# Gate1's and scale2's modulation moved from the heads to the first projections, with the first heads' parts in other buffers

## The chip, the core and the metric

The kernel runs on one core of a Trainium2 chip. The metric is the time of one execution in microseconds of the device. Matrix products run on TensorE (PE in the rows), with the weight loads as a row of their own (PEld); elementwise work runs on VectorE (DVE) and ScalarE (ACT); SyncE (SP) issues the DMAs.

## What is computed

One trunk layer over 512 positions of 1024 channels, in float32: two parallel branches, a merge by learned gates, and a squared-ReLU MLP. A modulation vector of six parts is computed from `c` first.

```python
mod = (c_act @ w_ada[l] + b_ada[l])[:, None, :]
shift1, scale1, gate1, shift2, scale2, gate2 = jnp.split(mod, N_MOD, axis=-1)

h = rms_norm(x) * (1.0 + scale1) + shift1
proj = h @ w_in[l]
xr, gr, q, k, v, gm = jnp.split(proj, [o1, o2, o3, o4, o5], axis=-1)
xr = causal_depthwise_conv(xr, conv_w[l], conv_b[l])
y_rnn = rg_lru(xr, ...) * jax.nn.gelu(gr)
q = apply_rope(rms_norm(q) * q_norm_gain[l], cos, sin)
k = apply_rope(rms_norm(k) * k_norm_gain[l], cos, sin)
y_attn = diff_attention(q, k, v, lam, subln_gain[l], lam_init)

gates = jax.nn.sigmoid(gm).reshape(B, S, N_BRANCH, D_MODEL)
merged = gates[:, :, 0] * (y_rnn @ w_proj_rnn[l]) + gates[:, :, 1] * (y_attn @ w_proj_attn[l])
x = x + gate1 * (merged @ w_out[l])
h2 = rms_norm(x) * (1.0 + scale2) + shift2
ff = jnp.square(jax.nn.relu(h2 @ w_ff1[l])) @ w_ff2[l]
x = x + gate2 * ff
```

Shift1 and scale1 are needed for the very first product, gate1 only behind `w_out`, scale2 only behind that.

## The kernel before

Everything is kept with channels on the 128 partitions and the 512 positions along the row, or the other way round for queries, keys and values. A float32 product is made of three products of a high part and a low part: `load_w` (L114) loads a 128x1024 block of weights (512 KB, DMA on SP), ScalarE casts it to the high part `wh` (L122), VectorE subtracts to get the low part `wl` (L123), and `mm3` (L127) issues three matmuls of 512 columns (L129, L130, L131) for each 128x128 block. One such block of weights, called a unit here, is 24 matmuls.

The stages, in the order in which they run: the x-branch `xr` (7 blocks in seven banks at once, then `xr7`), with shift1 and scale1 computed beside it by `ada_halves`; the first quarter of queries and keys (`qk_quarter(0)`, four units, which serves heads 0 and 1); the gelu gates `gr`, eight units, with the convolutions beside them; the first half of the values (`v_half(0)`, four units) with the RG-LRU gates (`gates`, L433, matmuls on `xch`, `xcl` into two banks `pg0`, `pg1`) and the transposes of the first queries and keys (`qk_transpose(0)`) between; then the heads. `heads()` yields after each small step of the attention, and `fill()` walks `PLAN`, in which letters stand for units: `g`, `m` merge gates (`gm`), `s` the scans, `q`, `t` further quarters of queries and keys, `v` the other values, `p` the products with `w_proj_rnn`. Behind them stand `pa` (the attention's projection), `wo`, and the MLP.

A column of the modulation vector is a dot product on VectorE of 1024 weights per partition with `c`. `ada_chunk(j, k)` (L184) does it with one instruction (L188) on a tile of 128x1024 in the pool "w" of 3 buffers, which the weights use too. `ada_halves(j, k)` (L191) does it with two instructions (L200), one behind the other, on tiles of 128x512 with tag "q" (12 buffers), in which from the gates on the parts of queries and keys live. `ADA` is (2, 4): part 2 is gate1, part 4 is scale2. `fill()` issues `ada_chunk(2, n)` with each step `p` and `ada_chunk(4, n)` with each step `m`; parts 3 and 5 have their own place beside `pa` and in the MLP.

`qk_transpose` makes for each of four groups a bank by four transposes, a high part `qh` (ScalarE, L549) and a low part `ql` (VectorE), and DMAs copy the halves of both to `qs`, `kh` and `kl` (L555, L556, L562, L563). A buffer of `qh` or `ql` is free again when its copies have landed. Both take tag "t" (4 buffers), which `xch` and `xcl` of the gates take too. Tag "a" has 6 buffers; `ig` of the gates (L445) and the attention's tiles take it. The banks `pg0`, `pg1` have tag "sc" (2 buffers), which the scores of the attention take too.

The order on each engine is made by a scheduler that goes by the order of the code and by its own estimates of when an instruction can start; the cast and the subtraction of `load_w` are put ahead of other work by `tc.high_priority(HP)`. So an instruction that is moved in the code can shift others on every engine.

Of the kernel before, what the change touches and what calls it, by code (L numbers as in the profile page):

```python
# [17 lines left out]
F32R = mybir.dt.float32r  # L18
# [9 lines left out]
KC = D // P  # L28
# [13 lines left out]
ADA = (2, 4)  # L42
# [11 lines left out]
def build(tc, out, x, xT_in, c, pos, vecs, reps, ada, w_xr, w_xr7, w_qk, w_v, w_gr, w_gm, w_lru,  # L54
# [4 lines left out]
    with ExitStack() as es:  # L59
# [11 lines left out]
        def slot(tag, bufs, name, dt=F32):  # L71
            return (big if tag in "mh" else mix).tile([P, S], dt, name=name, tag=tag, bufs=bufs)

        def t_(name, dt=F32, tag="t"):
            return (tmp if tag == "t" else mix).tile([P, S], dt, name=name, tag=tag,
                                                     bufs=dict(t=B_T, a=B_A, r=B_R)[tag])
# [31 lines left out]
        def f32(t):  # L108
            return t.bitcast(F32)
# [32 lines left out]
        def split_l(dst, src, h):  # L142
            return nc.vector.tensor_tensor(dst, src, f32(h), op=ALU.subtract)
# [40 lines left out]
        def ada_chunk(j, k):  # L184
            col = j * 8 + k
            w = wpool.tile([P, D], F32, name=f"ada{col}", tag="w", bufs=3)
            nc.sync.dma_start(w, ada[j, k])
            nc.vector.tensor_tensor_reduce(w, w, cb, 1.0, bada[:, col:col + 1], op0=ALU.mult,  # L188
                                           op1=ALU.add, accum_out=mod[:, col:col + 1])
# [234 lines left out]
        def conv(n):  # L424
            cw = lambda j: vec[:, V_CW + n * 4 + j:V_CW + n * 4 + j + 1]
            xc = slot("y", B_Y, f"xc{n}")
            nc.scalar.activation(xc, xr[n], AF.Identity, bias=vcol(V_CB, n), scale=cw(3))
            for sft in (1, 2, 3):
                nc.vector.scalar_tensor_tensor(xc[:, sft:], xr[n][:, :S - sft], cw(3 - sft), xc[:, sft:],
                                               op0=ALU.mult, op1=ALU.add)  # L430
            return xc

        def gates(n, xc, prev):  # L433

            xh = t_(f"xch{n}", F32R)
            nc.scalar.copy(xh, xc)
            xl = t_(f"xcl{n}", F32R)
            split_l(xl, xc, xh)
            c0 = slice(n % 4 * P, (n % 4 + 1) * P)
            pg = [bank(f"pg{j}_{n}", "sc", 2) for j in range(2)]  # L440
            for j in range(2):
                mm3(pg[j], wg[j][n // 4][0][:, c0], wg[j][n // 4][1][:, c0], xh, xl, True, True)
            r = slot("y", B_Y, f"r{n}")
            after(nc.scalar.activation(r, pg[0], AF.Sigmoid, bias=vcol(V_BA, n)), prev)
            ig = t_(f"ig{n}", tag="a")  # L445
            after(nc.scalar.activation(ig, pg[1], AF.Sigmoid, bias=vcol(V_BX, n)), prev)
            nc.vector.tensor_tensor(xc, ig, xc, op=ALU.mult)
            th = slot("m", B_M, f"th{n}")
            last = nc.scalar.activation(th, r, AF.Tanh, scale=sp4[:, n:n + 1])
            return r, xc, th, last  # L450
# [28 lines left out]
        def run(gen):  # L479
            while True:  # L480
                try:
                    next(gen)
                except StopIteration as e:
                    return e.value
# [24 lines left out]
        def qk_quarter(qt):  # L509

            pss = yield from token_major(w_qk[qt], f"qk{qt}_")
            s2 = tiny(f"qs{qt}", 32)
            rot = []
            v4 = lambda t: t.rearrange("p (m g d) -> p m g d", m=2, g=4)
            g8 = lambda t: t.rearrange("p (a b) -> p a b", b=64)
            for t in range(TB):
                raw = t_(f"raw{qt}_{t}", tag="r")
                nc.scalar.copy(raw, pss[t])
                rot.append(raw)
            for t in range(TB):  # L520
                raw = rot[t]
                sqt = t_(f"qsq{qt}_{t}", tag="r")
                nc.scalar.activation(sqt, raw, AF.Square)
                nc.vector.tensor_reduce(s2[:, t * 8:t * 8 + 8], g8(sqt), axis=AX.X, op=ALU.add)
                r4, s4 = v4(raw), v4(sqt)
                for hf in range(2):
                    a, b = slice(hf * 32, hf * 32 + 32), slice(32 - hf * 32, 64 - hf * 32)
                    nc.vector.tensor_tensor(s4[:, :, :, a], r4[:, :, :, b],
                                            st[:, t, :, None, a].to_broadcast([P, 2, 4, 32]), op=ALU.mult)
                nc.vector.tensor_tensor(r4, r4, ct[:, t, :, None, :].to_broadcast([P, 2, 4, 64]), op=ALU.mult)  # L530
                nc.vector.tensor_tensor(raw, raw, sqt, op=ALU.add)
            rq = tiny(f"rq{qt}", 32)
            rsqrt(rq, s2, 32, 1.0 / 64, EPS, f"rq{qt}")
            for t in range(TB):
                nc.vector.tensor_tensor(g8(rot[t]), g8(rot[t]),
                                        rq[:, t * 8:t * 8 + 8, None].to_broadcast([P, 8, 64]), op=ALU.mult)
            return rot

        def qk_transpose(qt, rot):


            res = []
            half = [slice(0, 64), slice(64, 128)]
            for j in (0, 2, 1, 3):
                pt = bank(f"qT{qt}_{j}", "tp", 1)
                for t in range(TB):
                    nc.tensor.transpose(pt[:, t * P:(t + 1) * P], rot[t][:, j * P:(j + 1) * P], ident)
                th = t_(f"qh{qt}_{j}", F32R)
                nc.scalar.copy(th, pt)  # L549
                tl = t_(f"ql{qt}_{j}", F32R)  # L550
                split_l(tl, pt, th)
                for m in range(2):
                    if j < 2:
                        st_ = slot("q", B_Q, f"qs{qt}_{j}_{m}", F32R)
                        nc.sync.dma_start(f32(st_)[half[0]], f32(th)[half[m]])  # L555
                        nc.sync.dma_start(f32(st_)[half[1]], f32(tl)[half[m]])  # L556
                        res.append(st_)
                    else:
                        pair = []
                        for x_, nm_ in ((th, "kh"), (tl, "kl")):  # L560
                            st_ = slot("q", B_Q, f"{nm_}{qt}_{j}_{m}", F32R)
                            nc.sync.dma_start(f32(st_)[half[0]], f32(x_)[half[m]])  # L562
                            nc.sync.dma_start(f32(st_)[half[1]], f32(x_)[half[m]])  # L563
                            pair.append(st_)
                        res.append(pair)
            return [((res[0], res[1]), (res[2], res[3])), ((res[4], res[5]), (res[6], res[7]))]
# [82 lines left out]
        xr = [evac_xr(n, xr_ps[n]) for n in range(NK)]  # L649
        xr.append(evac_xr(NK, project(w_xr7, h, "xr7")))  # L650
        wg = lru_weights()
        qk0 = run(qk_quarter(0))
        gel, xcs = [], []
        for n in range(KC):
            gel.append(gelu_block(n))
            xcs.append(conv(n))
        lg = []
        gv = v_half(0)
        for n in range(KC):
            if n % 2 == 0:  # L660
                next(gv)
            lg.append(gates(n, xcs[n], gel[-1][1]))
            if n == QT0:
                qk0 = qk_transpose(0, qk0)
        v0 = run(gv)
# [19 lines left out]
        def fill():  # L685

            rot = {}
            for group in PLAN.split("/"):
                for op in group.split():
                    o, n = op[0], int(op[1:])  # L690
                    if o == "g":
                        gate0(n)
                    elif o == "s":
                        hs = lru_scan(n, lg[n][0], lg[n][1], sqs[-1])
                        yr.append(y_rnn(n, hs, gel[n][0]))
                    elif o == "q":
                        rot[n] = yield from qk_quarter(n)
                    elif o == "t":
                        qks[n] = qk_transpose(n, rot.pop(n))
                    elif o == "v":  # L700
                        vs[n] = yield from v_half(n)
                    elif o == "p":
                        proj_rnn(n)
                        ada_chunk(ADA[0], n)
                    elif o == "m":
                        th1.append(gate(KC + n, slot("y", B_Y, f"thg{KC + n}")))
                        ada_chunk(ADA[1], n)
                if o not in "qv":
                    yield

# [48 lines left out]
        for n in range(KC):  # L759
            pp = project(w_pa[n], y_att, f"pa{n}")  # L760
            ada_chunk(3, n)
            th = t_(f"mg{n}")
# [12 lines left out]
        for n in range(KC):  # L775
# [3 lines left out]
            t = slot("m", B_M, f"x1_{n}")  # L779
# [47 lines left out]
        for k in range(KC):  # L827
            t = t_(f"h2f{k}")
# [278 lines left out]
```

## Time and profile before

| | us |
|---|---|
| runs | 893.14, 896.8, 897.4 |
| median | 896.8 |
| profiled execution | 894.77 |
| its span in the trace | 893.0 |
| PE busy | 867.7 (97%) |
| DVE busy | 657.4 (74%) |
| ACT busy | 448.3 (50%) |

The span is the time from the first to the last recorded instruction; 1.8 us of the profiled execution lie around it. The rows use the engine names above; a name such as `pg<-xch,wgh` is the output and the inputs of an instruction, without buffer numbers. A bracket at the end of a row, `[2.06 <-ACT xch L436]`, says that the engine stood idle for 2.06 us before it, and what ended the wait. Times in rows are counted from the start of the span.

### The profile page before, as it was taken

How to read it: one execution, taken by the hardware profiler on the slowest of the kernel's cores; microseconds unless marked ns; L12 is line 12 of the kernel's file. 1: busy time of each engine (PE TensorE's matmuls, PEld its weight loads, DVE VectorE, ACT ScalarE, POOL GpSimd, SP SyncE). 2: the span in 40 equal slices, each digit the busy share in tenths (PEclk: the TensorE clock that was granted, in tenths of full speed). 3: DMA queues.
4: the chain of work that ended last, by engine and by line, in shares of the span. 5: the costliest groups of instructions: out<-in, count | busy, mean ns of one | idle time of the engine just before them, and what ended most of it. 6: DMA issues, size and time to landing. Idle time of an engine off the chain costs nothing.

```text
span 893.0 us, 11189 instructions
## 1 busy us (share of the span) xinstructions
PE 867.7 (97%) x4012; PEld 707.0 (79%) x4012; DVE 657.4 (74%) x1227; ACT 448.3 (50%) x748; POOL 2.2 (0%) x40
## 2 busy tenths in 40 slices
PE   6999999999999999999999999989999999999988
PEld 3888888687878878877778888878888888888867
DVE  6972983499969855895868566879646883876597
ACT  6663544895536533534543343746545544553541
POOL 0000000000000000000000000000000000000000
PEclk9999999999999999999999999999999999999999
DMA  8932236321255474448745332772421342233002
GB/s 318 353 142 97 92 116 144 120 70 48 95 127 158 137 213 146 142 136 206 246 155 183 135 119 78 273 237 95 163 99 48 118 142 95 72 117 118 1 1 94
DMA packets 54874, 121.56 MB, mean 136 GB/s; under 512 B 5666, under 2 KB 23202, under 8 KB 54820
## 3 DMA queue, kind: packets, MB, share of 16 engines
q1 hardware_dynamic: 54820, 120.87, 41.9%
q8 instruction: 31, 0.51, 0.2%
q14 instruction: 23, 0.19, 0.1%
HBM read 106.17 MB, written 2.10 MB: 121 GB/s over the span
## 4 chain that ended last, share of the span: by engine, by line
PE 74%; DVE 16%; DMA 5%; ACT 2%; issue 2%; SPq 0%; DVEq 0%; ACTq 0%
PE f L129 5%; PE f L130 5%; PE f L131 5%; DMA ada<-in_ada 3%; DVE wl L123 3%; PE X L131 3%; PE X L130 3%; PE X L129 3%; PE qk L131 2%; PE qk L129 2%; PE qk L130 2%; PE xr L129 2%; PE xr L131 2%; PE xr L130 2%; PE wo L130 2%
## 5 line engine op out<-in xcount | busy, mean ns | idle before, releaser
L122 ACT CAST wh<-w 128x1024 fp32r<-128x1024 f32 (+1 forms) x113 | 117.9, 1043 | 214.6 <-issue 56.2
L123 DVE TENSOR_TENSOR wl<-w,wh 128x1024 fp32r<-128x1024 f32 (+1 forms) x113 | 137.0, 1213 | 87.7 <-ACT wh L122 86.6
L129 PE MATMUL f<-h2h,wh 128*128 128x512 f32 x240 | 93.0, 390 | 2.3 <-ACT wh L122 2.3
L131 PE MATMUL f<-h2h,wl 128*128 128x512 f32 x240 | 93.5, 390 | 0.4 <-DVE wl L123 0.4
L130 PE MATMUL f<-h2l,wh 128*128 128x512 f32 x240 | 93.2, 389 | 0.0
L129 PEld LDWEIGHTS f<-h2h,wh 128*128 128x128 f32 x240 | 45.1, 188 | 12.0 <-ACT wh L122 2.7
L131 PEld LDWEIGHTS f<-h2h,wl 128*128 128x128 f32 x240 | 45.1, 188 | 10.0 <-DVE wl L123 0.8
L188 DVE CUSTOM_DVE_ANT_0 ada<-ada,cb,bada 128x1024 f32<-128x1024 f32 x32 | 41.0, 1281 | 16.1 <-DMA ada<-in_ada 16.1
L130 PEld LDWEIGHTS f<-h2l,wh 128*128 128x128 f32 x240 | 45.1, 188 | 9.3
L131 PE MATMUL gm<-hh,wl 128*128 128x512 f32 x128 | 51.3, 401 | 0.0
L129 PE MATMUL gm<-hh,wh 128*128 128x512 f32 x128 | 51.1, 399 | 0.0
L130 PE MATMUL gm<-hl,wh 128*128 128x512 f32 x128 | 50.9, 398 | 0.0
L129 PE MATMUL qk<-wh,hh 128*128 128x512 f32 x128 | 50.8, 398 | 0.0
L131 PE MATMUL qk<-wh,hl 128*128 128x512 f32 x128 | 50.6, 395 | 0.0
L130 PE MATMUL qk<-wl,hh 128*128 128x512 f32 x128 | 50.2, 393 | 0.0
L588 ACT ACTIVATE e<-e,nm 128x128 f32<-128x128 f32 (+3 forms) x64 | 35.8, 561 | 28.7 <-DVE nm L586 28.4
L905 DVE TENSOR_TENSOR p_1l<-b,p_1h 128x1024 fp32r<-128x1024 f32 x27 | 33.0, 1223 | 21.8 <-ACT p_1h L904 21.8
L904 ACT CAST p_0h<-b 128x1024 fp32r<-128x1024 f32 x27 | 28.5, 1054 | 27.2 <-PE X L131 14.0
L904 ACT CAST p_1h<-b 128x1024 fp32r<-128x1024 f32 x27 | 28.3, 1050 | 27.3 <-PE f L130 24.5
L905 DVE TENSOR_TENSOR p_0l<-b,p_0h 128x1024 fp32r<-128x1024 f32 x27 | 33.0, 1222 | 11.7 <-ACT p_0h L904 11.6
L948 DVE TENSOR_TENSOR b<-b,b 128x1024 f32<-128x1024 f32 x32 | 38.7, 1220 | 0.1
L586 DVE CUSTOM_DVE_ANT_0 e<-sc,mask 128x128 f32<-128x128 f32 (+3 forms) x64 | 30.3, 486 | 10.4 <-PE sc L581 10.4
(438 smaller groups left out, 2169.8 us busy)
## 6 DMA issues: line engine op xcount, KB each, us to landing
ada<-in_ada SPq DMA_DIRECT2D x32, 512.0 KB, 4.2
w<-in_w_ff SPq DMA_DIRECT2D x32, 512.0 KB, 3.2
b<-in_w_ff SPq DMA_DIRECT2D x32, 512.0 KB, 3.5
ada<-in_ada SPq DMA_DIRECT2D x32, 256.0 KB, 5.8
w<-in_w_qk SPq DMA_DIRECT2D x16, 512.0 KB, 3.3
w<-in_w_gm SPq DMA_DIRECT2D x16, 512.0 KB, 3.6
w<-in_w_gr SPq DMA_DIRECT2D x8, 512.0 KB, 3.2
w<-in_w_v SPq DMA_DIRECT2D x8, 512.0 KB, 3.2
```

Source lines behind the costliest of these rows:

```text
L122: i_w = nc.scalar.copy(wh[:, :n], w[:, :n])
L123: nc.vector.tensor_tensor(wl[:, :n], w[:, :n], f32(wh)[:, :n], op=ALU.subtract)
L129: nc.tensor.matmul(ps, lh, rh, start=first, stop=False, skip_group_check=more)
L130: nc.tensor.matmul(ps, lh, rl, start=False, stop=False, skip_group_check=more)
L131: nc.tensor.matmul(ps, ll, rh, start=False, stop=last, skip_group_check=more)
L188: nc.vector.tensor_tensor_reduce(w, w, cb, 1.0, bada[:, col:col + 1], op0=ALU.mult, op1=ALU.add, accum_out=mod[:, col:col + 1])
L586: nc.vector.tensor_tensor_reduce(e[:, :n], ps[m][:, :n], mask[:, S - n:], 1.0, 1e30, op0=ALU.add, op1=ALU.min, accum_out=nm)
L588: nc.scalar.activation(e[:, :n], e[:, :n], AF.Exp, bias=nm, scale=-1.0, accum_out=sums[:, m:m + 1])
L904: nc.scalar.copy(v4(wh), v)
L905: nc.vector.tensor_tensor(v4(wl), v, f32(v4(wh)), op=ALU.subtract)
L948: nc.vector.tensor_tensor(d, d, s_, op=ALU.add)
```

## The change

Three edits. `qk_transpose(0)` takes `qh` and `ql` of the first quarter from tag "a" instead of "t". The sixteen `ada_chunk` calls in `fill()` go. In their place stand `ada_halves(2, 0..7)`, two beside each of the four units of the first queries and keys, `ada_halves(4, 0..3)` beside the units 4 to 7 of `gr`, and `ada_halves(4, 4..7)` behind the first gates. Sixteen instructions of 128x1024 become 32 of 128x512, and sixteen DMAs of 512 KB become 32 of 256 KB, all in buffers of tag "q".

```diff
--- before.py
+++ after.py
@@ -545,9 +545,10 @@
                 pt = bank(f"qT{qt}_{j}", "tp", 1)
                 for t in range(TB):
                     nc.tensor.transpose(pt[:, t * P:(t + 1) * P], rot[t][:, j * P:(j + 1) * P], ident)
-                th = t_(f"qh{qt}_{j}", F32R)
+                tag = "t" if qt else "a"
+                th = t_(f"qh{qt}_{j}", F32R, tag)
                 nc.scalar.copy(th, pt)
-                tl = t_(f"ql{qt}_{j}", F32R)
+                tl = t_(f"ql{qt}_{j}", F32R, tag)
                 split_l(tl, pt, th)
                 for m in range(2):
                     if j < 2:
@@ -649,17 +650,27 @@
         xr = [evac_xr(n, xr_ps[n]) for n in range(NK)]
         xr.append(evac_xr(NK, project(w_xr7, h, "xr7")))
         wg = lru_weights()
-        qk0 = run(qk_quarter(0))
+        qk0 = qk_quarter(0)
+        for n in range(4):
+            next(qk0)
+            for i in range(2):
+                ada_halves(ADA[0], 2 * n + i)
+        qk0 = run(qk0)
         gel, xcs = [], []
         for n in range(KC):
             gel.append(gelu_block(n))
             xcs.append(conv(n))
+            if n >= 4:
+                ada_halves(ADA[1], n - 4)
         lg = []
         gv = v_half(0)
         for n in range(KC):
             if n % 2 == 0:
                 next(gv)
             lg.append(gates(n, xcs[n], gel[-1][1]))
+            if n == 0:
+                for i in range(4, KC):
+                    ada_halves(ADA[1], i)
             if n == QT0:
                 qk0 = qk_transpose(0, qk0)
         v0 = run(gv)
@@ -701,10 +712,8 @@
                         vs[n] = yield from v_half(n)
                     elif o == "p":
                         proj_rnn(n)
-                        ada_chunk(ADA[0], n)
                     elif o == "m":
                         th1.append(gate(KC + n, slot("y", B_Y, f"thg{KC + n}")))
-                        ada_chunk(ADA[1], n)
                 if o not in "qv":
                     yield
 
```

The line numbers behind L547 are higher by one in the changed kernel up to L652. In the order of the instructions a name such as `pg1_3` has a block's number, and a bracket says which semaphores an instruction waits for.

**PE, values and gates.** Before the change, all matmuls of the gates 2 and 3 (`pg0_2` to `pg1_3`) stand together behind the last row of the values `v0_3`, and `gm0`, the first merge gate, follows:

```order
L131 MATMUL v0_3_1268<-wh24_1547,hl7_558 128x512
L129 MATMUL pg0_2_1443<-xch2_1439,wgh0_0_756 128x512 [waits Activation_49]
L129 MATMUL pg1_2_1444<-xch2_1439,wgh1_0_766 128x512
L130 MATMUL pg0_2_1443<-xcl2_1441,wgh0_0_756 128x512 [waits DVE_49]
L131 MATMUL pg0_2_1443<-xch2_1439,wgl0_0_757 128x512
L130 MATMUL pg1_2_1444<-xcl2_1441,wgh1_0_766 128x512
L131 MATMUL pg1_2_1444<-xch2_1439,wgl1_0_767 128x512
L129 MATMUL pg0_3_1462<-xch3_1458,wgh0_0_756 128x512 [waits Activation_49]
```

After it, they stand between the rows of the values' third unit (`wh23`, `wl23`), with the last transposes `qT0_3`:

```order
L131 MATMUL pg0_3_1574<-xch3_1570,wgl0_0_757 128x512
L131 MATMUL v0_0_1349<-wh23_1591,hl4_402 128x512
L547 MATMUL qT0_3_1500<-ident_99,raw0_0_955 128x128 [waits DVE_49]
L547 MATMUL qT0_3_1500<-ident_99,raw0_1_957 128x128
L547 MATMUL qT0_3_1500<-ident_99,raw0_2_959 128x128
L547 MATMUL qT0_3_1500<-ident_99,raw0_3_961 128x128
L129 MATMUL v0_0_1349<-wh23_1591,hh5_450 128x512
L130 MATMUL v0_0_1349<-wl23_1592,hh5_450 128x512
L129 MATMUL pg1_3_1575<-xch3_1570,wgh1_0_766 128x512 [waits Activation_49]
```

The gates moved forward by some 40 rows. The row of `pg1_3` waits for ScalarE, since its bank is the one that `ig2` reads.

**ACT, the same place.** Before the change, `xch2` and `xch3` wait for DMAs (the copies out of the `qh` and `ql` whose buffers they take over):

```order
L122 CAST wh25_1660<-w25_1658 128x1024 [waits DMAHW0_49,PE_49]
L549 CAST qh0_3_1393<-qT0_3_1388 128x512 [waits DMAHW6_49,DMAHW3_49,DMAHW7_49,DMAHW2_49,DVE_49]
L436 CAST xch2_1439<-xc2_1070 128x512 [waits DMAHW6_49,DMAHW0_49,DVE_49]
L122 CAST wh26_1760<-w26_1758 128x1024 [waits DMAHW1_49,PE_49]
L444 ACTIVATE r2_1451<-pg0_2_1443,vec_93 128x512 [waits PE_49]
L446 ACTIVATE ig2_1453<-pg1_2_1444,vec_93 128x512 [waits PE_49]
L449 ACTIVATE th2_1456<-r2_1451,sp4_624 128x512 [waits Activation_49]
L436 CAST xch3_1458<-xc3_1108 128x512 [waits DMAHW5_49,DMAHW7_49,DMAHW1_49,DVE_49]
```

After it, no `xch` of this stretch waits for a DMA, and `ig2` does:

```order
L550 CAST qh0_1_1490<-qT0_1_1485 128x512 [waits DVE_49,PE_49]
L444 ACTIVATE r2_1563<-pg0_2_1555,vec_93 128x512 [waits PE_49]
L436 CAST xch4_1619<-xc4_1202 128x512 [waits DVE_49,PE_49]
L449 ACTIVATE th2_1568<-r2_1563,sp4_624 128x512 [waits Activation_49]
L444 ACTIVATE r3_1582<-pg0_3_1574,vec_93 128x512 [waits PE_49]
L550 CAST qh0_3_1505<-qT0_3_1500 128x512 [waits DMAHW4_49,DMAHW2_49,PE_49]
L449 ACTIVATE th3_1587<-r3_1582,sp4_624 128x512 [waits Activation_49]
L436 CAST xch5_1638<-xc5_1247 128x512 [waits DVE_49,PE_49]
L446 ACTIVATE ig2_1565<-pg1_2_1556,vec_93 128x512 [waits DMAHW6_49,DMAHW3_49,DMAHW7_49,DMAHW2_49,DVE_49]
L446 ACTIVATE ig3_1584<-pg1_3_1575,vec_93 128x512 [waits DVE_49,PE_49]
L122 CAST wh25_1772<-w25_1770 128x1024 [waits DMAHW0_49,PE_49]
```

The wait for the copies moved from `xch` to `ig2`, which now shares tag "a" with them, and the casts of the weights `wh25` stand behind it.

**PE, the last heads.** Before the change, the transposes `yT5` of head 5's result stand directly ahead of `aT6_1` of head 6; both use the one bank of tag "tp":

```order
L131 MATMUL gm11_4383<-hh7_554,wl60_4380 128x512
L641 MATMUL yT5_4133<-ident_99,o15_3999 128x128 x4
L603 MATMUL aT6_1_4142<-ident_99,e6_1_0_4063 128x128 x2
L614 MATMUL po6_4054<-vs1_0_3021,aTs6_1_4145 128x128
L614 MATMUL po6_4054<-vs1_1_3023,aTs6_1_4145 128x128
```

After it, eight matmuls of the merge gate 11 stand between them:

```order
L642 MATMUL yT5_4221<-ident_99,o15_4090 128x128 x4
L131 MATMUL gm11_4462<-hh1_238,wl60_4459 128x512
L129 MATMUL gm11_4462<-hh2_294,wh60_4458 128x512
L130 MATMUL gm11_4462<-hl2_298,wh60_4458 128x512
L131 MATMUL gm11_4462<-hh2_294,wl60_4459 128x512
L129 MATMUL gm11_4462<-hh3_346,wh60_4458 128x512
L130 MATMUL gm11_4462<-hl3_350,wh60_4458 128x512
L131 MATMUL gm11_4462<-hh3_346,wl60_4459 128x512
L129 MATMUL gm11_4462<-hh4_398,wh60_4458 128x512
L604 MATMUL aT6_1_4230<-ident_99,e6_1_0_4154 128x128 x2
```

The transposes of head 5 moved forward against the merge gate's matmuls.

## Rows read from the trace of the kernel before

**Rows 1.** The page: busy time, share of the span and instructions of each engine.
```profile
PE 867.7 (97%) x4012; PEld 707.0 (79%) x4012; DVE 657.4 (74%) x1227; ACT 448.3 (50%) x748; POOL 2.2 (0%) x40
```

**Rows 2.** Windows: stretch, length, busy PE, PEld, DVE, ACT, POOL, PEclk, DMA, GB/s.
```profile
60.00:87.00 27.00, 27.00 (x121) 22.37 (x120) 7.41 (x8) 8.97 (x12) 0.00 (x0) 1.00 0.39 137
87.00:120.20 33.20, 33.20 (x148) 27.48 (x148) 32.11 (x58) 18.35 (x26) 0.00 (x0) 1.00 0.27 95
```

**Rows 3.** Timeline of VectorE: start, length, line, operation, tiles, wait before it.
```profile
46.15 0.75 DVE L200 CUSTOM_DVE_ANT_0 ada<-ada,cb,adah 128x512 f32<-128x512 f32 x1
...
46.82 0.75 DVE L200 CUSTOM_DVE_ANT_0 ada<-ada,cb,bada 128x512 f32<-128x512 f32 x1
...
86.99 1.23 DVE L123 TENSOR_TENSOR wl<-w,wh 128x1024 fp32r<-128x1024 f32 x1 [4.21 <-ACT wh L122]
...
120.23 1.22 DVE L123 TENSOR_TENSOR wl<-w,wh 128x1024 fp32r<-128x1024 f32 x1
```

**Rows 4.** Timeline of TensorE, gelu gates to gates.
```profile
124.23 0.39 PE L131 MATMUL gr<-hh,wl 128*128 128x512 f32 x1
...
144.01 0.40 PE L129 MATMUL v<-wh,hh 128*128 128x512 f32 x1
...
159.43 0.73 PE L129 MATMUL pg<-xch,wgh 128*128 128x512 f32 x2 [2.06 <-ACT xch L436]
```

**Rows 5.** Windows around three places, columns as in rows 2.
```profile
160.00:164.00 4.00, 4.00 (x11) 3.03 (x11) 0.79 (x2) 2.94 (x6) 0.00 (x0) 0.57 0.81 321
180.00:220.00 40.00, 39.22 (x191) 31.26 (x190) 39.03 (x98) 29.49 (x69) 0.00 (x0) 1.00 0.20 66
600.00:602.00 2.00, 1.06 (x5) 0.87 (x6) 1.08 (x1) 2.00 (x3) 0.00 (x0) 1.00 0.74 246
```

**Rows 6.** Timeline of ScalarE, gates.
```profile
145.17 0.58 ACT L549 CAST qh<-qT 128x512 fp32r<-128x512 f32 x1
...
157.58 0.68 ACT L446 ACTIVATE ig<-pg,vec 128x512 f32<-128x512 f32 x1
...
158.77 0.61 ACT L436 CAST xch<-xc 128x512 fp32r<-128x512 f32 x1
```

**Rows 7.** Timeline of SP's queue: the tenth copy of the first queries and keys.
```profile
148.03 0.59 SPq L563 DMA_DIRECT2D kh<-qh  x1
```

**Rows 8.** DMA issues: tiles, count, KB each, us from issue to landing.
```profile
kh<-qh SPq DMA_DIRECT2D x32, 128.0 KB, 2.4
```

**Rows 9.** Timeline of TensorE, heads: each wait, and one in the MLP.
```profile
331.05 0.45 PE L581 MATMUL sc<-kh,qs 128*128 128x384 f32 x1 [0.54 <-DVE nm L586]
...
384.99 0.50 PE L131 MATMUL pr<-yh,wl 128*128 128x512 f32 x1 [0.45 <-DVE wl L123]
...
387.60 0.44 PE L603 MATMUL aT<-ident,e 128*128 128x128 f32 x2 [0.27 <-DVE yal L645]
...
422.62 0.44 PE L603 MATMUL aT<-ident,e 128*128 128x128 f32 x2 [1.56 <-DVE yal L645]
...
423.56 0.71 PE L614 MATMUL po<-vs,aTs 128*128 128x128 f32 x4 [0.50 <-ACT aTs L606]
...
433.11 0.44 PE L581 MATMUL sc<-kh,qs 128*128 128x384 f32 x1 [0.42 <-DVE nm L586]
...
442.60 0.66 PE L641 MATMUL yT<-ident,o 128*128 128x128 f32 x4 [0.83 <-DVE o L634]
...
461.34 0.63 PE L641 MATMUL yT<-ident,o 128*128 128x128 f32 x4 [0.71 <-DVE o L634]
...
600.94 0.50 PE L129 MATMUL f<-h2h,wh 128*128 128x512 f32 x1 [2.29 <-ACT wh L122]
```

**Rows 10.** Line 188 in 290 to 450: VectorE's waits there, and one instruction.
```profile
L188 DVE CUSTOM_DVE_ANT_0 ada<-ada,cb,bada x17: 1264/1279/1289, 295.7 to 445.4; 128x1024 f32<-128x1024 f32 x17
...
  DMA ada<-in_ada: 7.4, 6
...
440.24 1.29 DVE L188 CUSTOM_DVE_ANT_0 ada<-ada,cb,bada 128x1024 f32<-128x1024 f32 x1 [0.94 <-DMA ada<-in_ada]
```

## The prediction

> **What bounds the kernel now.** I read the page's busy times first: TensorE works for 867.7 us of the span of 893.0, VectorE for 657.4, ScalarE for 448.3 [rows 1]. The span ends sooner only if a wait of TensorE, or a stretch at its lower clock, gets shorter, and only 25 us of waits are there to take. Then I read windows by stage, to see which engine has room where the change puts work: beside the first queries VectorE is busy for 7.41 of 27.00 us, beside the gates gr1 to gr6 for 32.11 of 33.20 [rows 2]. Third, TensorE's timeline between 120 and 465 us: each row with a bracket is time that the change can give back or add [rows 4, 9]. Last, what ScalarE, the copies' queue and VectorE's own waits show at those places [rows 3, 6, 7, 8, 10].
>
> **Part one, 32 halves beside queries and gelu gates.** A half takes 0.75 us, and the next starts 0.67 us after it [rows 3], so 32 take 21.4 us of VectorE. In the order, up to six of them stand ahead of the low part of one weight unit. A unit is 24 matmuls; 148 matmuls fill 33.20 us, 0.224 each [rows 2], so a unit lasts 5.4 us. Six halves and one low part (1.15 us start to start) take 5.2 us, and VectorE idles 19.6 of the 27.00 us beside the queries: nothing is late there. The tight place lies behind. Between the low parts of gr1 (86.99) and gr7 (120.23) [rows 3] the order holds the same instructions as before and six halves more: 4.0 us, where VectorE had 33.20 − 32.11 = 1.1 us free [rows 2]. So the low part of gr7 is 2.9 us late and ends at 120.23 + 1.22 + 2.9 = 124.35, while the third matmul of that unit, the first to need it, starts at 124.23 [rows 4]. That costs 0.1 to 0.2 us; I take 0.2, with 0 and 0.9 as ends (0.9 if one more half, 0.67, is in the way). The sixteen added DMAs ask for no more bytes, and in both stretches the DMA engines are busy for 0.27 to 0.39 [rows 2], so I cost them at nothing; if the weights behind them on SP came late, each low part would be late by the same amount.
>
> **Part two, values and gates.** Before, TensorE waits 2.06 us at 159.43 for the cast `xch` [rows 4], which the copies of the first queries hold up through the buffers of tag "t"; behind the wait, the granted clock is 0.57 over the next 4 us, though TensorE is busy all the time [rows 5]. At half speed, 0.43 of 4 us is 1.7 us lost. Together 3.8 us, which the change removes, since those copies no longer hold these buffers.
>
> But the order shows a new wait. `pg1_3` takes the bank that `ig2` reads, and `ig2` now takes the buffer of the first key part and so waits until its copies have landed. TensorE comes to `pg1_3` at about 148.1: the matmul at 144.01 [rows 4] stands 14 matmuls (3.1 us) and two groups of four transposes ahead of it, the latter at 0.35 to 0.63 us (a group of four shows 0.63 [rows 9]). The last copy that `ig2` waits for is the tenth, issued at 148.03 [rows 7]; with 2.4 us from issue to landing [rows 8] it is there at 150.4. ScalarE alone would come to `ig2` at about 149.7: from `qh` at 145.17 eight instructions, each some 0.55 to 0.60 us after the last (157.58 to 158.77 is two) [rows 6]. So `ig2` runs from 150.4 to 151.1 and TensorE waits 3.0 us; if the copies land early, 2.1. Whether the clock falls behind it: the nearest row is the same place, where it fell after 2.06 us of idling [rows 4, 5], so I take 1.7 us more. The other end is no fall: at 600.94 TensorE waited 2.29 us [rows 9], and the clock of 600 to 602 reads 1.00 [rows 5]. I take 4.7 for the new against 3.8 for the old: 0.9 us slower, with ends of −1.7 (2.1 without a fall) and +1.2. On ScalarE, `wh25` and the `r` of the next gates are queued behind `ig2`; the values' third and fourth units, whose casts stand ahead, don't wait for it.
>
> The Trainium skill says in "TensorE: Matmul & The Clock Gate", section "What's actually happening", that the throttled state is the default and activity releases it, so that an engine that idles falls back to 1.2 GHz. By it alone the new hole costs its 1.7 us, and the sum stays as below, 891.7; by the row at 600.94, which shows a hole of this size without a fall, the sum would be 890.0. The two waits of before stand on either side of that rule.
>
> **Part three, the heads.** Sixteen chunks leave VectorE, each 1.28 us (1.20 start to start) [rows 10], 19 us in all, and with them six waits for their DMAs, 7.4 us [rows 10], in which everything behind a chunk stood still: at 440.24 it waited 0.94 us, worked 1.29 us, and behind it in the order stands head 6's norm, for which TensorE then waits 0.83 us at 442.60 [rows 9, 10]. I expect these waits of TensorE to go [rows 9]: 384.99 (0.45), 387.60 (0.27), 433.11 (0.42), 442.60 (0.83), 461.34 (0.71), in which a chunk stands shortly ahead on VectorE, together 2.68; and 422.62 (1.56) with 423.56 (0.50), 2.06, which the order takes away, because eight matmuls (1.8 us) now stand between `yT5` and `aT6_1`. That is 4.74. The small wait at 331.05 (0.54) had no chunk just ahead of it; such waits come with any order of these rows, and I take one new one of that size: −4.2. The bounds are −4.74 and −2.1 (the two order-led waits come back elsewhere).
>
> **Sum.** +0.2 + 0.9 − 4.2 = −3.1, from 894.77 to 891.7 for an execution like the profiled one. The median of the runs is 896.8, 2.0 above it, and would go to 893.7. The two differ by less than the runs do (893.14 to 897.4); I take 893.0, between them.
>
> **Rivals.** *More is gained.* The new wait is 2.1 us and the clock stays up (−1.7), and no new small wait comes (−4.74, +0.2): −6.2, 888.5. For it speaks the row at 600.94; against it the fall at the same place before. *Slower: VectorE becomes the bound of the first head.* In the order, the first scores come 28 rows of TensorE earlier, so 28 × 0.224 = 6.3 us of matmuls no longer stand ahead of them. In 180 to 220 us VectorE is busy for 39.03 of 40.00 us [rows 5]: the heads' start goes by VectorE, and the matmuls taken from there were cover. If all of it is exposed, TensorE waits 6.3 us more: −3.1 + 6.3 = +3.2, 898.0, and with one more fall of the clock (1.7) +4.9, 899.7. It decides from 3.1 us exposed on. Against it: TensorE is busy for 39.22 of these 40.00 us [rows 5], and matmuls that moved ahead of the scores have others in their place behind them. *The order's gain doesn't last:* the waits of `yT5` and `aTs` (2.06) appear at another head: −1.0, 893.7 for the profiled execution.
>
> **Chances.** A measurement of this kernel can tell some 0.5%, 4.5 us, from no change. Forecast (−3.1) 0.42, more gained 0.30, VectorE as the bound 0.15, the order's gain lost 0.13. Faster by over 0.5% are most of the second (0.26) and the low edge of the first (0.05): 0.31. Slower by over 0.5%: two thirds of the third, 0.10, and 0.01 of the rest: 0.11. The rest, 0.58, is within 0.5%. The range of 887.5 to 898.5 runs from 1.0 under the second case to the third's lower price with little over it; it leaves out the third's second half and the tails.
>
> **What would show it.** A wait of TensorE for `ig` of about 3 us before `pg` between 147 and 152, and the granted clock in the 4 us behind it (about 0.57, or 1.00); no wait for `xch` near 159. The low part of gr7 ending at about 124.3. No line 188 on VectorE before `pa`, and TensorE without waits for `yal`, `o` and `wl` between 380 and 465. The windows of the first head: if TensorE is busy for under 36 of the 40 us behind the first scores, the third case is there. The prediction is wrong if waits of more than 3 us come up in a stage that no term names, above all if weights arrive late between 60 and 125 us.

## The result and the profile after

The changed kernel takes 885.4 us (median of four runs, 883.4 to 888.8) against 895.7 us of the kernel before in the same comparison: a ratio of 0.989, 95% interval 0.985 to 0.993. That is 10.4 us, where 3.1 were forecast, and below the forecast range. The profiled execution took 885.12 us, its span is 883.3 us, 9.6 us less than the 893.0 of before (883.35 and 892.97 unrounded). The page's first part, which answers to [rows 1]:

```profile
span 883.3 us, 11249 instructions
## 1 busy us (share of the span) xinstructions
PE 864.3 (98%) x4012; PEld 706.4 (80%) x4012; DVE 660.6 (75%) x1259; ACT 448.3 (51%) x748; POOL 2.2 (0%) x40
```

TensorE's idle time fell from 25.3 to 19.0 us. VectorE is a little busier than before: the 32 halves cost more than the 16 chunks, and yet the end comes sooner. To see where, I cut the span at three instructions of TensorE's timeline: the first matmul of the values, the first scores, and the first matmul of `pa`. In the kernels with tag "a" for the first quarter, 28 matmuls that stood ahead of the first scores stand behind them; I count these 6.4 us (28 × 0.2275, the usual step between matmuls of 512 columns) in the gates' stage for all kernels alike. Where these matmuls fill short delays in the heads, the count credits that to the heads.

| kernel | to the first value matmul | values and gates | heads | `pa` to the end | span |
|---|---|---|---|---|---|
| before | 129.2 | 46.7 | 281.6 | 435.4 | 893.0 |
| changed | 129.3 | 42.7 | 275.2 | 436.1 | 883.3 |
| difference | 0.0 | −3.9 | −6.4 | +0.7 | −9.6 |

So 3.9 us came from the gates, which were forecast to lose 0.9, and 6.4 from the heads, forecast at 4.2. The stage behind `pa` hides a gain of 1.0 us: behind the waits of the MLP's end the granted clock fell in this execution, for 1.7 us, and did not in that of before. Windows of the changed kernel, columns as in [rows 2]:

```profile
160.00:164.00 4.00, 4.00 (x18) 3.08 (x17) 1.47 (x2) 2.90 (x5) 0.00 (x0) 1.00 0.60 241
180.00:220.00 40.00, 38.16 (x195) 30.67 (x194) 39.88 (x97) 26.08 (x60) 0.00 (x0) 1.00 0.19 66
850.00:860.00 10.00, 7.19 (x28) 5.11 (x27) 10.00 (x13) 2.10 (x2) 0.00 (x0) 0.90 0.01 2
860.00:870.00 10.00, 10.00 (x41) 7.84 (x41) 7.70 (x10) 3.90 (x4) 0.00 (x0) 0.92 0.08 26
```

The first row answers to 160:164 in [rows 5], where the clock read 0.57: it is 1.00 now. In the last two rows 0.10 and 0.08 of 10 us each are lost, 1.8 us together.

The wait that the prediction put at the gates is not there. TensorE's timeline:

```profile
148.14 0.40 PE L130 MATMUL v<-wl,hh 128*128 128x512 f32 x1
148.37 0.40 PE L129 MATMUL pg<-xch,wgh 128*128 128x512 f32 x1
```

ScalarE's timeline of the same stretch, with `r3` and `ig2`:

```profile
147.44 0.69 ACT L444 ACTIVATE r<-pg,vec 128x512 f32<-128x512 f32 x1
...
151.08 0.69 ACT L446 ACTIVATE ig<-pg,vec 128x512 f32<-128x512 f32 x1 [1.26 <-DVE xcl L143]
```

The `pg` at 148.37 is the second product of gates 3, for which a wait until the end of `ig2` was forecast (at 151.1; it came at 151.8). It comes 0.24 us behind the end of `r3` (147.44 + 0.69 = 148.13) and 0.23 behind the matmul ahead of it: no wait. Since it starts 2.7 us before `ig2` does, it can't be in the bank that `ig2` reads; of the two banks it has the one that `r3` had read. The sentence under the order of TensorE, and the step built on it, were wrong.

The hold on `ig2` itself is there. Its bracket names VectorE, whose `xcl` had ended at 150.54; what came last was a copy on SP's queue, 2.4 us from issue to landing, so landed at 150.93:

```profile
148.53 0.60 SPq L564 DMA_DIRECT2D kh<-qh  x1
```

All waits of TensorE between 130 and 500 us that carry a bracket, which answer to [rows 9]:

```profile
182.04 0.44 PE L604 MATMUL aT<-ident,e 128*128 128x128 f32 x2 [0.19 <-DVE e L596]
...
190.80 0.52 PE L604 MATMUL aT<-ident,e 128*128 128x128 f32 x3 [0.66 <-DVE e L596]
...
195.23 0.63 PE L604 MATMUL aT<-ident,e 128*128 128x128 f32 x4 [0.44 <-DVE e L596]
...
209.71 0.66 PE L642 MATMUL yT<-ident,o 128*128 128x128 f32 x4 [0.38 <-DVE o L635]
...
217.60 0.63 PE L604 MATMUL aT<-ident,e 128*128 128x128 f32 x4 [0.17 <-DVE e L596]
...
246.21 0.30 PE L547 MATMUL qT<-ident,raw 128*128 128x128 f32 x1 [0.74 <-DVE raw L535]
...
452.10 0.39 PE L129 MATMUL pa<-yah,wh 128*128 128x512 f32 x1
452.97 0.50 PE L130 MATMUL pa<-yal,wh 128*128 128x512 f32 x1 [0.49 <-DVE yal L646]
```

From 250 us to `pa` there is none left. The last two rows show what a wait costs: the starts are 0.87 us apart, where matmuls follow each other at 0.23, so 0.64 us are lost for a bracket of 0.49. A restart costs 0.15 us on top, and the eight waits of [rows 9] that went had that cost too.

### The profile page after: what moved, and what is told of

The parts are those of the page before. It is cut to its first block, busy times and chain, and to the rows that moved or that the text cites. A ratio compares the mean times of both kernels' runs of the same rounds, so it can differ in the third digit from the quotient of the medians.

```text
span 883.3 us, 11249 instructions
## 1 busy us (share of the span) xinstructions
PE 864.3 (98%) x4012; PEld 706.4 (80%) x4012; DVE 660.6 (75%) x1259; ACT 448.3 (51%) x748; POOL 2.2 (0%) x40
## 4 chain that ended last, share of the span: by engine, by line
PE 84%; DVE 9%; DMA 3%; ACT 2%; issue 1%; SPq 0%; DVEq 0%; ACTq 0%
PE f L129 5%; PE f L130 5%; PE f L131 5%; PE X L131 3%; PE gm L129 3%; PE X L129 3%; PE X L130 3%; PE gm L130 3%; PE gm L131 2%; PE qk L131 2%; PE qk L129 2%; PE qk L130 2%; PE sc L582 2%; PE xr L129 2%; PE pr L129 2%; PE po L615 2%
## 5 line engine op out<-in xcount | busy, mean ns | idle before, releaser
L188 DVE CUSTOM_DVE_ANT_0 ada<-ada,cb,bada 128x1024 f32<-128x1024 f32 x16 | 20.5, 1284 | 14.7 <-DMA ada<-in_ada 14.7
```

## The experiments

Theories at the start: the two edits add up, the tag giving the gates' stage and the moved modulation giving the heads (theory 1); against it, that the gain in the heads comes from the shifted order, or that a wait of the predicted kind is there but hidden. All ratios are to the kernel before on the same chip. The stages of each profiled execution are in one table behind the runs, with what the lower clock cost on average.

**The tag alone.**

```diff
+                tag = "t" if qt else "a"
-                th = t_(f"qh{qt}_{j}", F32R)
+                th = t_(f"qh{qt}_{j}", F32R, tag)
...
-                tl = t_(f"ql{qt}_{j}", F32R)
+                tl = t_(f"ql{qt}_{j}", F32R, tag)
```

> The kernel before with one edit: the first quarter's high and low parts take tag "a"; the chunks of gate1 and scale2 stay in the heads. Theory 1 (the copies' hold on the casts is the whole loss of the gates' stage, and nothing takes its place): the 2.06 us wait near 159 and the 0.57 clock behind it go, no new wait comes, the waits between 380 and 465 stay; 3.9 us off the span of 893.0, so 889.1. Theory 2 (as predicted: the second bank of gates 3 waits for ig): a wait of 3.0 us near 148 and a fall of the clock, 893.9.

894.1 us, 0.998 (0.9965 to 0.9996): 2.1 us by the medians, where theory 1 gave 3.9 and theory 2 none. The place did what theory 1 says: no wait near 159, none for `ig`, and the stage takes 42.7 us as in the changed kernel. But the waits of the heads' end stay, and the clock falls behind them. TensorE's timeline of this kernel:

```profile
418.57 0.44 PE L604 MATMUL aT<-ident,e 128*128 128x128 f32 x2 [1.56 <-DVE yal L646]
419.51 0.71 PE L615 MATMUL po<-vs,aTs 128*128 128x128 f32 x4 [0.50 <-ACT aTs L607]
```

And the window behind them, columns as in [rows 2]:

```profile
420.00:424.00 4.00, 3.96 (x18) 3.42 (x18) 3.96 (x11) 3.12 (x6) 0.00 (x0) 0.58 0.80 267
```

These are the two waits of 422.62 and 423.56 in [rows 9], of the same length, with a fall (0.58 for 4 us, 1.7 us) that the profiled execution of before did not have; two more lie behind `pa`. So theory 1 holds for the place. For the size the recorded clocks help: span times one minus the mean granted clock is what an execution lost to the lower clock, and that is 3.9 us on average over the twelve executions here, against 3.8 of the kernel before. The fall that went at the gates is made up elsewhere, and the 2.1 us left are about the wait (2.06) and its restart.

**The moved modulation alone.**

```diff
-                tag = "t" if qt else "a"
+                tag = "t"
```

> The changed kernel with its tag "a" undone: only the modulation is moved. Theory 1 (the two edits add up): the 2.06 us wait and the low clock of the gates stay, the waits of 380 to 465 go; 6.4 us off, 886.6. Theory 2 (the gain in the heads comes from the other order that the tag brings): under 4 us off, over 889.

888.4 us, 0.9917 (0.9901 to 0.9932), a span of 886.5, where theory 1 gave 886.6. 7.9 and 2.1 us by the medians make 10.0, against 10.4 for both edits (9.0 on a second chip): within the intervals they add up. That the span fits to 0.1 us is luck in part: the heads gave 5.2 us, not 6.4, and one thing was not as expected. The wait of 2.06 us before `pg` is there, and the clock behind it does not fall (timeline of TensorE and window of this kernel):

```profile
159.36 0.73 PE L129 MATMUL pg<-xch,wgh 128*128 128x512 f32 x2 [2.06 <-ACT xch L436]
...
160.00:164.00 4.00, 4.00 (x17) 2.95 (x17) 1.20 (x3) 3.38 (x7) 0.00 (x0) 1.00 0.81 309
```

**No modulation of gate1 and scale2 at all.** Only their bias is copied.

```diff
         mod = const.tile([P, 48], F32, name="mod")
+        for j in ADA:
+            nc.vector.tensor_copy(mod[:, j * 8:j * 8 + 8], bada[:, j * 8:j * 8 + 8])
...
-                        ada_chunk(ADA[0], n)
...
-                        ada_chunk(ADA[1], n)
```

> The kernel before without any work for gate1 and scale2: no DMAs, no dot products, only their bias is copied (parts 2 and 4 of the modulation are left out). Theory 1 (the halves beside queries and gelu gates cost about 0.2 us): the same as the kernel with the modulation moved alone, within 0.5 us, 886.4. Theory 2 (the halves cost a hidden part of what the heads gain): 1.5 us or more below that one, under 885.

889.2 us, 0.9921 (0.9904 to 0.9938), against 0.9917 with the halves beside the queries: no difference by the medians, as theory 1 has it. The lower clock blurs this: it cost these executions 3.8 us on average and those with the halves 2.2, and in the profiled pair this kernel's heads are 1.1 us shorter. So the 21 us of added work on VectorE cost 0 to 1.6 us, and the lower end of theory 2 is not excluded.

**The bank that the prediction had read.** Each of the two gate products gets a bank of its own.

```diff
-            pg = [bank(f"pg{j}_{n}", "sc", 2) for j in range(2)]
+            pg = [bank(f"pg{j}_{n}", f"sc{j}", 1) for j in range(2)]
...
-            ps = [bank(f"sc{hd}_{i}_{m}", "sc", 2) for m in range(2)]
+            ps = [bank(f"sc{hd}_{i}_{m}", f"sc{m}", 1) for m in range(2)]
```

> The changed kernel, with a bank of its own for each of the two gate products (and for each of the two score maps), so that the second product of gates 3 takes the bank that ig2 reads, as the prediction had it. In the order it then stands 17 rows later on TensorE. Theory 1: TensorE comes there at 152.2, ig2 ends at 151.8, so no wait and the time of the changed kernel, 883.3, within 1 us. Theory 2 (the price of the prediction): a wait of up to 3 us and a fall of the clock, 885.5 to 888.

886.6 us, 0.9889 (0.9872 to 0.9906), the changed kernel's ratio. TensorE's and ScalarE's timelines of this kernel:

```profile
153.09 0.39 PE L129 MATMUL pg<-xch,wgh 128*128 128x512 f32 x1
...
151.56 0.69 ACT L446 ACTIVATE ig<-pg,vec 128x512 f32<-128x512 f32 x1 [1.42 <-DMA kh<-qh]
```

The product starts without a wait; `ig2` ends at 152.25, released by the landing copy as forecast. So the time of `ig2` was about right (150.4 to 151.1 forecast, 151.1 to 151.8 in the changed kernel), and the hole still isn't there: with the bank as assumed, the scheduler puts the product 17 rows further back.

**The chunks in the heads without their DMAs, and without their work.** Neither kernel computes gate1 and scale2. First the dot product of a resident tile:

```diff
-            nc.sync.dma_start(w, ada[j, k])
-            nc.vector.tensor_tensor_reduce(w, w, cb, 1.0, ...
+            if j in ADA:
+                src = cb
+            else:
+                src = w
+                nc.sync.dma_start(w, ada[j, k])
+            nc.vector.tensor_tensor_reduce(w, src, cb, 1.0, ...
```

> The kernel before, its sixteen chunks of gate1 and scale2 still in the heads, but each is a dot product of a resident tile, with no DMA (parts 2 and 4 of the modulation are wrong numbers). VectorE's 19 us of work stay, its 7.4 us of waits for DMAs go. Theory D (the heads lose by VectorE standing still for the DMAs): most of the gain of the kernel with the modulation moved alone, 888 to 890. Theory W (they lose by the work, whenever it comes): within 2 us of the kernel before, 894 to 896.

891.8 us, 0.9965 (0.9948 to 0.9981): 3.4 us of the 7.9, between the two forecasts. Then the DMA with 16 of 1024 columns of work:

```diff
-            nc.vector.tensor_tensor_reduce(w, w, cb, 1.0, ...
+            m = 16 if j in ADA else D
+            nc.vector.tensor_tensor_reduce(w[:, :m], w[:, :m], cb[:, :m], 1.0, ...
```

> The kernel before, its sixteen chunks with their DMAs of 512 KB still in the heads, but each dot product covers 16 of 1024 columns (parts 2 and 4 of the modulation are left out but for those). VectorE's work of 19 us goes, its waits for the DMAs stay. Theory D: within 2 us of the kernel before, 894 to 896. Theory W: near the kernel with the modulation moved alone, 888 to 890. If both matter, each gives about half, 892.

896.7 us, 1.0017 (1.0000 to 1.0034), near theory D: nothing gained by taking some 17 us of work off VectorE, and the 1.5 us lost are about what the lower clock took (5.4 us on average, against 3.8). What VectorE waits for at the chunks' line in this kernel, in the form of [rows 10]:

```profile
L189 DVE CUSTOM_DVE_ANT_0 ada<-ada,cb,bada x17: 215/230/1285, 294.3 to 443.2; 128x16 f32<-128x16 f32 x16, 128x1024 f32<-128x1024 f32 x1
...
  DMA ada<-in_ada: 9.7, 5
```

Two waits in TensorE's timeline of it:

```profile
413.64 0.66 PE L642 MATMUL yT<-ident,o 128*128 128x128 f32 x4 [1.17 <-DVE o L635]
415.87 0.44 PE L604 MATMUL aT<-ident,e 128*128 128x128 f32 x2 [1.57 <-DVE yal L646]
```

VectorE waits 9.7 us there instead of 7.4. By the stages, the heads gained 4.1 us of the 5.2 without the DMAs, and 1.3 without the work (282.0 less its fall of 1.7, against 281.6): the DMAs mattered more. But that VectorE stood in its order before a DMA that had not landed (theory D) is not shown to be the whole of it. The runs take two more things away with it. In the kernel before, ScalarE's casts wait three times for the DMAs of weights between 325 and 430 us, 6.0 us in all, and in the version without the chunks' DMAs not once. And the order changes: in the last two rows `yT` and `aT` stand side by side, as in [rows 9] at 422.62, and the wait between them is as long (1.57 and 1.56 us), with no wait for a chunk near it in the kernel before; with the modulation moved alone, eight matmuls of `gm` stand between them and there is no wait. So 2.06 us of the heads' gain are a matter of the order, and these runs don't separate it from the DMAs and the work.

**Other buffers in the heads.** The chunks as halves in tag "r", so that they take no buffer from the weights:

```diff
-                w = slot("q", B_Q, f"ada{col}_{i}")
+                if j in ADA:
+                    w = t_(f"ada{col}_{i}", tag="r")
+                else:
+                    w = slot("q", B_Q, f"ada{col}_{i}")
...
-                        ada_chunk(ADA[0], n)
+                        ada_halves(ADA[0], n)
...
-                        ada_chunk(ADA[1], n)
+                        ada_halves(ADA[1], n)
```

> The kernel before, its chunks of gate1 and scale2 still in the heads, but as halves of 128x512 in the buffers of tag "r" (those of the raw queries and keys), not in the three buffers that the weights use. VectorE's work stays (32 x 0.67 us), and the DMAs stay. Theory B (the chunks' DMAs come late because they take turns with the weights for three buffers): VectorE's 7.4 us of waits go and most of what the version without DMAs gained comes, 891 to 892.5. Theory Q (a DMA in the heads is late whatever its buffer): within 2 us of the kernel before, 894 to 896.

905.2 us, 1.011 (1.008 to 1.014): slower by 10 us, which neither theory gave. SP's queue in this kernel, and its wait there for the dot product of an earlier half (total, times, longest):

```profile
397.51 5.04 SPq L201 DMA_DIRECT2D ada<-in_ada  x2
...
SPq L201 <- DVE mod L203: 4.4, 1, 4.4
```

Two waits in its timeline of TensorE:

```profile
419.06 0.39 PE L584 MATMUL sc<-kh,qs 128*128 128x256 f32 x1 [2.51 <-DVE nm L589]
...
425.49 1.11 PE L644 MATMUL yT<-ident,o 128*128 128x128 f32 x4 [2.64 <-DVE o L637]
```

And its window of 420 to 430:

```profile
420.00:430.00 10.00, 5.71 (x17) 4.22 (x18) 7.09 (x32) 5.61 (x21) 0.00 (x0) 0.50 0.77 214
```

SP stood 5 us at the halves' DMAs around 400, ahead of the copies of the last queries and keys (404 to 422), VectorE waited 3.1 us for a half at 410, and TensorE idled 4.3 of 10 us at half clock. On average the lower clock cost these executions 10.7 us, 6.7 more than those of the kernel before on that chip, which is most of the 10. Whether the waits of the kernel before come from the weights' buffers, this run can't say; it only shows that buffers whose next DMA waits for a dot product on a full VectorE are worse. The trace of the kernel before says more. Two of SP's waits in it, 290 to 450 us, in the same form:

```profile
SPq L118 <- DVE mod L188: 30.3, 7, 5.7
...
SPq L187 <- DVE wl L123: 13.2, 4, 6.2
```

Seven loads of weights (L118) waited for the end of a chunk's dot product, and four chunks (L187) for a subtraction of `load_w`: they do take turns for the three buffers. The longest wait of VectorE for a chunk, 4.19 us until 358.00, is one of the four: its DMA was issued at 353.84.

**A better version.** The changed kernel's longest wait outside the start is 2.10 us in the MLP, behind the eight chunks of gate2, which stand in a row. TensorE's timeline of the changed kernel:

```profile
590.02 0.50 PE L129 MATMUL f<-h2h,wh 128*128 128x512 f32 x1 [2.10 <-ACT wh L122]
```

ScalarE's, with the cast that this matmul waits for:

```profile
588.92 1.04 ACT L122 CAST wh<-w 128x1024 fp32r<-128x1024 f32 x1 [2.42 <-DMA w<-in_w_ff]
```

And SP's queue, with the chunks' DMAs ahead of the weights':

```profile
580.99 2.54 SPq L187 DMA_DIRECT2D ada<-in_ada  x2
585.07 6.51 SPq L118 DMA_DIRECT2D w<-in_w_ff  x4
```

The edit:

```diff
-            if qd == 0:
-                for n in range(KC):
-                    ada_chunk(5, n)
+            for n in range(2 * qd, 2 * qd + 2):
+                ada_chunk(5, n)
```

> The changed kernel, and the eight chunks of gate2, which stand in a row beside the first quarter of the MLP, spread two to each of its four quarters. TensorE waits 2.1 us for wh at 590 in the changed kernel, and this cast waits 2.4 us for a DMA that stands on SP behind the chunks' DMAs. Theory 1 (the row of chunks is the cause): the wait goes, 2.3 us off (2.1 and a restart of 0.17), and 1.8 us more where the clock would have fallen there: 881.5 to 883. Theory 2 (the stage's own loads are the cause): no difference, 885.4.

882.4 us, 0.9856 (0.9832 to 0.9879), and the changed kernel beside it on that chip:

> The changed kernel once more, on the chip of the three others. The same as before: a ratio of 0.989, 885 to 886, and in its trace the same waits; only the places where the granted clock falls may differ, at 1.7 to 1.8 us each.

886.2 us, 0.9893 (0.9867 to 0.9919). So the spread chunks take another 3.8 us off by the medians; theory 1 holds (the lower clock makes 1.2 of it, 1.8 against 3.0 us on average on that chip). The window of 575 to 595 shows it, first in the changed kernel (its first trace):

```profile
575.00:595.00 20.00, 17.90 (x80) 14.47 (x79) 16.74 (x23) 7.87 (x12) 0.00 (x0) 1.00 0.74 252
```

Then with the chunks spread:

```profile
575.00:595.00 20.00, 20.00 (x90) 16.53 (x89) 13.82 (x16) 10.51 (x14) 0.00 (x0) 1.00 0.27 86
```

The DMA share went from 0.74 to 0.27, and TensorE has no hole. Once more on a third chip:

> The changed kernel with gate2's chunks spread, once more, on the chip of the two others: 882.4 as before, a ratio of 0.9856, within 1 us.

882.4 us, 0.9857 (0.9834 to 0.988). The second trace of the changed kernel has two waits more than the first, 0.29 us at 257.07 and this one, and a fall of the clock behind the MLP's wait at 591:

```profile
124.96 0.50 PE L131 MATMUL gr<-hh,wl 128*128 128x512 f32 x1 [1.01 <-DVE wl L123]
```

This is the tight place of part one, with the upper end of its price (0.9). It shows in three of the seven traces with halves: 1.01 here, 0.77 with the banks apart, 0.33 with more cover.

**More cover for the first head**, on top of the spread chunks:

```diff
-UNITS = [4.25, 5.25, ...
+UNITS = [5.25, 5.25, ...
```

> The changed kernel with gate2's chunks spread over the four quarters of the MLP, and one more unit of filling work (24 matmuls, 5.4 us) beside head 0 (4.25 to 5.25). The changed kernel's new waits at the first head (0.19, 0.66, 0.44, 0.38 and 0.17 us between 180 and 218) come from 28 matmuls fewer ahead of its scores. Theory 1 (cover is what they lack): they go, 1.5 to 2.5 us less than without this edit. Theory 2 (VectorE bounds the head, whatever stands on TensorE): they stay, or new waits come where the unit is missing; within 1 us or slower.

883.8 us, 0.987 (0.9848 to 0.9893), against 882.4 for the kernel without it, within the intervals: no gain, theory 2. The waits of the first head stay (0.17, 0.64 and 0.45 us at 182.64, 191.40 and 196.97), and that for `o` grows to 0.67.

The stages of the profiled executions, cut as in the first table, with the falls of the clock that their windows show (a fall is a stretch at the lower clock; where no length is given it cost about 1.7 us). The last column is the mean over all executions on record with a clock of what the lower clock cost, in us; a fall in the last 4 us of a span is left out of the falls:

| kernel | values and gates | heads | `pa` to the end | falls | lower clock |
|---|---|---|---|---|---|
| before | 46.7 | 281.6 | 435.4 | gates | 3.8 |
| tag alone | 42.7 | 281.1 | 439.1 | heads, two behind `pa` | 3.9 |
| modulation alone | 45.3 | 276.4 | 435.6 | one behind `pa` | 2.2 |
| no modulation | 46.7 | 275.2 | 434.5 | gates, one behind `pa` | 3.8 |
| banks apart | 42.8 | 275.5 | 436.3 | one behind `pa` | 2.9 |
| chunks without DMA | 45.4 | 277.5 | 438.0 | two behind `pa` | 3.4 |
| chunks without work | 45.4 | 282.0 | 437.8 | heads, one behind `pa` | 5.4 |
| chunks in other buffers | 46.6 | 286.7 | 442.6 | gates, heads (6.8 us), two behind `pa` | 10.7 |
| changed | 42.7 | 275.2 | 436.1 | one behind `pa` | 2.8 |
| changed, spread | 42.8 | 275.5 | 432.6 | one behind `pa` | 1.9 |
| spread, more cover | 42.7 | 276.7 | 433.7 | one behind `pa` (3.4 us) | 2.3 |

## Why the prediction was wrong

**Part one was right.** It had the low part of gr7 2.9 us late at the third matmul, for 0.2 us with an end of 0.9. That part ran from 122.83 to 124.05, 2.6 us later than before, and the first matmul of the values came at 129.26 instead of 129.22, from a start 0.1 us earlier: 0.14 us. In the second trace the same place cost 1.0. The kernel without any halves comes to that matmul at 128.88, from a start 0.4 us earlier, so nothing else was lost there.

**Part two failed at one step: "`pg1_3` takes the bank that `ig2` reads".** It takes the bank that `r3` reads, four instructions earlier on ScalarE. Here the pool of two banks gave the product the bank that was released first in the order, not the next in turn; from names and a semaphore of ScalarE alone, `r3` and `ig2` can't be told apart. Everything else in that step held: the copies do hold `ig2` until 151, the casts `xch` are free, the old wait and its fall are gone. Without the false step the part reads −3.8, and −3.9 was measured in the profiled pair (on average of the runs the tag gave 2.1, since falls came elsewhere). This is 4.8 of the 6.6 us by which the profiled execution missed the sum; part three adds 2.7, and the rest of the kernel, with its fall of 1.7, takes 1.1 back. The lower end of the new wait, 2.1 us, comes to 2.3 by the prediction's own times; nothing hangs on it.

**Part three had the mechanism right and the size too small.** Every wait that was named went, the order-led pair too; that pair is gone in the kernel with the modulation alone and stays in that with the tag alone, so it went with the chunks. The brackets give: −4.74, −0.54 for the wait at 331.05, which went as well, +1.08 for the first heads, −0.06, and +0.49 for a new wait in `pa`: −3.8 in all, near the −4.2 of the sum. The stages lost 6.4 (heads) and 0.5 (`pa`, 44.9 to 44.5 us). The 3.1 us between are time that no bracket shows. Six waits fewer in all (thirteen before, seven after), at 0.15 to 0.2 for each restart, make 0.9 to 1.2 of them. The rest lies in delays too short for a bracket, which starts at 0.15 us: steps between matmuls that are 0.05 us or more longer than usual and have no bracket add up to 11.5 us in the heads before and 9.0 after (some 0.6 of the difference may be four matmuls that the trace of before lacks). A part of that came with the tag and not with the chunks: without its fall, the heads of the tag alone are 2.2 us shorter than before at the same sum of brackets (6.2 against 6.1). The rule used, that a wait costs its bracket, is the term that was mis-sized.

The reason given for these waits was half right. The prediction spoke of 19 us of work and 7.4 us of waits. As far as these runs show, the smaller number mattered more: 4.1 us of the heads went with the DMAs, 1.3 with the work, of 5.2 for both. How much of the 4.1 is VectorE standing still, how much late weights and how much the order is not shown.

**The rivals.** *More is gained* came nearest (−6.2 forecast for the profiled execution, −9.7 measured), but for another reason than its own: it had a hole of 2.1 us without a fall, and there was no hole. *VectorE bounds the first head* is there as a mechanism, at 1.1 us instead of 6.3 (five waits of 1.84 us instead of four of 0.76): VectorE is busy for 39.88 of the 40 us, TensorE for 38.16 instead of 39.22, and more cover didn't help. *The order's gain doesn't last* fell.

## What to carry to other kernels

A dot product that must wait for its own DMA can cost more by the DMA than by its work (here 4.1 against 1.3 us): put such work where the engine has idle time and buffers are free, and ask of each chunk whether its DMA has landed when its turn comes, and which loads stand behind it. When a wait is read from an order, find out which buffer or bank it is for before giving it a price, and if the order can't say, carry both cases with a chance each. When waits are added up, add a restart for each one, and compare the lengths of whole stages, since short delays have no bracket. Compare the mean clocks of the runs before crediting an edit with a fall that went in one trace. And look for the next row of large DMAs ahead of weights, since here the same remedy, applied to gate2, gave another 3.8 us.

## What was not expected of the hardware

The clock falls behind holes of about the same length in some executions and not in others. Behind the 2.06 us before `pg`, the window of 160 to 164 reads 0.57 in the kernel before, 0.58 in that without modulation and in that with the chunks in other buffers, and 1.00 in those with the modulation alone, the chunks without DMA and the chunks without work. The Trainium skill, "TensorE: Matmul & The Clock Gate", section "What's actually happening", has the throttled state as the default to which an idle engine returns; here three of six holes of one length at one place brought it back, and three did not. Most falls cost 1.7 us (one of 3.4 and one of 6.8 are in the table), and they make a good part of the spread between executions: four executions of the changed kernel had spans of 881.3, 883.3, 883.7 and 887.0 us at mean granted clocks of 0.999, 0.997, 0.998 and 0.994. A hole of 2 us is so a hole of 2 or of nearly 4 us, and a single profile can't say which.
